# A two-layer transformer kernel: the opening of each squared-ReLU MLP by ordinary products, with moved buffers and shifted weights

## The chip, the cores and the metric

One core of a Trainium2 chip. The metric is the device time of one execution, in microseconds (us). TensorE multiplies, VectorE (DVE), ScalarE (ACT) and GpSimd (POOL) work on tiles in the on-chip memory, and DMA queues load weights. Everything is in 32-bit floats: each operand is split into a high part and a low remainder, and one product is made as three (high by high, high by low, low by high).

## What is computed

Two transformer blocks over 512 positions of 1024 features. The second, which this change touches, has two layers: an even mixer (a gated part and stick-breaking attention), then an MLP; an odd mixer (an mLSTM in chunks), then a second MLP. Cut to what matters:

```python
def _sqrelu_mlp(h, w1, w2):
    return jnp.square(jax.nn.relu(h @ w1)) @ w2

def _odd_mixer(h, w_in, conv_w, conv_b, i_b, f_b, on_g, w_out):
    p = h @ w_in
    qk = jax.nn.silu(_causal_conv(p[..., :n_qk], conv_w, conv_b))
    ...
    hc = _mlstm(q, k, v, i_pre, f_pre)
    hc = _rmsnorm(hc, on_g.reshape(C_HEADS, C_V)).astype(h.dtype)
    y = (hc * jax.nn.sigmoid(og)).reshape(bsz, seq, MIX_W)
    return y @ w_out

# each layer: x = x + mixer(rmsnorm(x, g1)); x = x + mlp(rmsnorm(x, g2))
```

w1 is 1024 x 4096 and w2 is 4096 x 1024. The norm's factor per position goes through relu and square, so it can be put on at the end.

## The kernel before

X holds the activations as eight tiles of 128 features by 512 positions, X[0] to X[7]. The program is laid out by a planner: Python writes the operations, a scheduler gives each engine its own order, and pools of tiles decide where tiles lie. A tile that takes the place of an older one waits for the older one's last reader.

A plain gemm (`gemm_t_steps`) has eight weights m of 128 outputs. `load_w` fetches each (128 x 1024), ACT makes its high part wH (L198) and DVE, or POOL where `pool_l` or `B.lean` says so, the low part wL (L200). Per weight, TensorE does 24 products of 512 columns (`mm3`, L204) into one accumulator, and the result is evacuated: for od_out, DVE adds it to X[m] (L881), for ev_out at L1264; both then take up the sum of squares `ssq` (L314).

`sq_mlp(layer)` works through four chunks c of 1024 hidden features. In a chunk there are four pairs p, each 256 hidden features by two weights, and then the gemm with w2, whose eight results are scaled and added to X (L1042, L1043). A pair is computed by a seven-product scheme: 2 x 2 blocks of weights and activations, seven products q instead of eight, each of four steps i of three products of 256 columns, 84 in all. It needs sums of weight blocks (`Pairs.weights`: tiles wH/wL, vH/vL, uH/uL with the temporary `eb`) and sums of activation blocks. Those are made once for a layer, in `Pairs.__init__`: for each i of 0 to 3 four blocks t1, t2 (X times its gain, ACT, L912), e and f (sums, DVE, L915 to L921), all split into high (ACT, L284) and low (DVE, L285): gH/gL, aH/aL, fH/fL. The results of a pair are combined on DVE, passed through relu and square on ACT (`done`), and split into the ring `hd` of eight tiles, which w2 reads.

The first pair of the first chunk, the opening, goes step by step over i, so that it can begin when i = 0 is ready. `norm` computes the norm's factor from `ssq` with one product of the row means (`pg`), behind pair 3 of chunk 0.

The pools: `hq0` and `hq1` belong to the two MLPs. `od` holds the odd mixer's tiles, among them the activations s2 and v which od_out's gemm reads, and is closed behind od_out; `hq1` is opened then and takes the same memory. `gap(pool, n)` puts a small tile into a pool, so that the tiles behind it lie 4n bytes further; `OFF = 16` moves a weight tile by 16 floats, 64 bytes.

## Time and profile before

| what | us |
|---|---|
| time, median of 3 runs | 1919.21 (1918.03 to 1919.74) |
| the profiled execution | 1916.68 |
| its span | 1914.9 |
| TensorE busy | 1855.4 (97%) |
| DVE busy | 1227.1 (64%) |
| ACT busy | 868.5 (45%) |
| POOL busy | 142.0 (7%) |

All stretches below are times from the start of the profiled execution's span. Layer 0's MLP begins where ev_out's gemm ends, near 998, layer 1's where od_out's ends, near 1555.5. A matmul's shown time is longer than the distance to the next, since matmuls are pipelined; the distance of neighbouring starts, or the chain's time over the number, is what one costs. [...]

### The profile page before, as it was taken

Reading aid. Unit: us, or ns where it says so; the run is one execution under the profiler, and the core shown is the slowest. Engines: PE = TensorE matmul, PEld = TensorE weight load, DVE = VectorE, ACT = ScalarE, POOL = GpSimd, SP = SyncE. Lnnn points to the kernel's source line nnn. Section 1 sums busy time; section 2 is a strip of 40 time slices with the busy share of each in tenths; the row PEclk is TensorE's granted clock in tenths of the full one; section 3 lists DMA queues with packets and bytes.
Section 4 is the critical chain, followed back from the end, with each engine's and each line's share of the span. In section 5 each row is a group of like instructions: output and inputs, shape, how many; then the busy total and the mean of one; then the engine's idle time right before and its main releaser. Section 6 shows DMA issues by size and latency. Waiting matters only on the chain.

```text
span 1914.9 us, 24808 instructions
## 1 busy us (share of the span) xinstructions
PE 1855.4 (97%) x9722; PEld 1533.9 (80%) x9722; DVE 1227.1 (64%) x1899; ACT 868.5 (45%) x1374; POOL 142.0 (7%) x101
## 2 busy tenths in 40 slices
PE   7999999999999999999899999999999969999999
PEld 3777788888888887776679899898777859899897
DVE  4765668664444346667878758586835577858583
ACT  2455454342323245666556344354436445445351
POOL 1000010110000002325320000001201000000000
PEclk9999999999999999999999999999999979999999
DMA  7513247522332223211122324232231213324231
GB/s 246 162 50 113 89 167 263 188 81 96 99 99 99 91 96 116 66 56 56 44 89 89 103 85 135 86 111 85 94 100 42 88 55 104 115 88 136 70 122 55
DMA packets 61652, 197.60 MB, mean 103 GB/s; under 512 B 6904, under 2 KB 8490, under 8 KB 61536
## 3 DMA queue, kind: packets, MB, share of 16 engines
q1 hardware_dynamic: 57864, 190.34, 30.5%
q10 hardware_dynamic: 3672, 5.69, 1.0%
q8 instruction: 76, 1.25, 0.3%
q14 instruction: 40, 0.33, 0.1%
HBM read 193.86 MB, written 2.15 MB: 102 GB/s over the span
## 4 chain that ended last, share of the span: by engine, by line
PE 84%; DVE 10%; ACT 4%; issue 1%; DMA 1%; SPq 0%; DVEq 0%; ACTq 0%
PE acc L204 63%; PE pm L204 15%; PE pg L204 3%; PE po L204 3%; DVE s L1395 1%; DVE sl L1315 1%; PE pm L207 1%; DVE wL L200 1%; DVE ssq L314 1%; ACT wH L198 0%; DVE aL L285 0%; DMA oh<-ada 0%; DVE vL L285 0%; DVE sq L1042 0%; ACT sz L1333 0%
## 5 line engine op out<-in xcount | busy, mean ns | idle before, releaser
L204 PE MATMUL acc<-hd,wH 128*128 128x512 f32 (+1 forms) x1552 | 474.7, 388 | 0.0
L198 ACT ACTIVATE wH<-wraw 128x1024 fp32r<-128x1024 f32 (+1 forms) x240 | 246.5, 1029 | 474.0 <-PE acc L204 399.0
L200 DVE TENSOR_TENSOR wL<-wraw,wH 128x1024 fp32r<-128x1024 f32 (+1 forms) x205 | 242.0, 1182 | 171.6 <-ACT wH L198 169.0
L204 PEld LDWEIGHTS acc<-hd,wH 128*128 128x128 f32 x1552 | 290.0, 188 | 59.6 <-issue 1.0
L204 PE MATMUL acc<-aH,wH 128*128 128x512 f32 (+1 forms) x784 | 308.5, 395 | 6.1 <-ACT aH L348 5.7
L204 PE MATMUL acc<-aL,wH 128*128 128x512 f32 (+1 forms) x784 | 303.0, 386 | 2.5 <-DVE aL L349 2.5
L204 PE MATMUL acc<-aH,wL 128*128 128x512 f32 (+1 forms) x784 | 303.0, 386 | 0.0
L204 PE MATMUL acc<-hd,wL 128*128 128x512 f32 (+1 forms) x776 | 301.1, 388 | 0.8
L204 PEld LDWEIGHTS acc<-aH,wH 128*128 128x128 f32 x784 | 148.8, 190 | 43.2 <-issue 10.3
L204 PEld LDWEIGHTS acc<-aL,wH 128*128 128x128 f32 x784 | 148.9, 190 | 32.4 <-DVE aL L349 3.4
L204 PEld LDWEIGHTS acc<-aH,wL 128*128 128x128 f32 x784 | 148.8, 190 | 30.8 <-issue 1.2
L204 PEld LDWEIGHTS acc<-hd,wL 128*128 128x128 f32 x776 | 145.7, 188 | 33.7 <-DVE wL L200 4.2
L200 POOL TENSOR_TENSOR wL<-wraw,wH 128x1024 fp32r<-128x1024 f32 x38 | 96.1, 2532 | 940.8 <-ACT wH L198 919.9
L1042 DVE TENSOR_TENSOR sq<-acc,R 128x512 f32<-128x512 f32 x63 | 43.3, 687 | 87.5 <-PE acc L204 87.3
L285 DVE TENSOR_TENSOR hd<-rl,hd 128x512 fp32r<-128x512 f32 (+1 forms) x64 | 61.1, 956 | 49.2 <-ACT hd L284 49.1
L669 DVE SCALAR_TENSOR_TENSOR X<-acc,mod,X 128x512 f32<-128x512 f32 x32 | 24.0, 751 | 83.5 <-PE acc L204 83.5
L284 ACT ACTIVATE hd<-rl 128x512 fp32r<-128x512 f32 (+1 forms) x64 | 53.8, 841 | 41.0 <-DVE rl L851 40.7
L971 ACT ACTIVATE rl<-rl 128x512 f32<-128x512 f32 x64 | 36.8, 623 | 65.5 <-DVE rl L1008 61.8
L204 PE MATMUL acc<-s,wH 128*128 128x512 f32 (+1 forms) x208 | 65.8, 375 | 0.0
L204 PE MATMUL pm<-s,s 64*128 64x384 f32 (+7 forms) x160 | 55.7, 436 | 0.0
L284 ACT ACTIVATE vH<-wraw 128x1024 fp32r<-128x1024 f32 x32 | 33.9, 1059 | 41.7 <-DVE wraw L948 32.1
L204 PE MATMUL acc<-wH,aH 128*128 128x512 f32 x120 | 50.2, 418 | 1.8 <-DVE cp L1391 1.8
(417 smaller groups left out, 3693.1 us busy)
## 6 DMA issues: line engine op xcount, KB each, us to landing
wraw<-mlp SPq DMA_DIRECT2D x128, 512.0 KB, 3.5
wraw<-w SPq DMA_DIRECT2D x64, 512.0 KB, 3.4
wraw<-ada SPq DMA_DIRECT2D x32, 512.0 KB, 4.3
wraw<-w_in SPq DMA_DIRECT2D x30, 512.0 KB, 3.9
oh<-ada SPq DMA_DIRECT2D x32, 256.0 KB, 4.7
wraw<-od_in SPq DMA_DIRECT2D x16, 512.0 KB, 3.4
wraw<-ev_in SPq DMA_DIRECT2D x12, 512.0 KB, 3.5
X<-x SPq DMA_DIRECT2D x16, 256.0 KB, 4.5
```

Source lines behind the costliest of these rows:

```text
L198: nc.scalar.activation(h[:, :n], r[:, :n], AF.Copy)
L200: (nc.gpsimd if pool_l else nc.vector).tensor_tensor(l[:, :n], r[:, :n], h[:, :n], op=OP.subtract)
L204: self.weave.placed(self.nc.tensor.matmul(out, w, x, start=start, stop=stop), out, x)
L207: self.weave.placed(self.nc.tensor.transpose(out, x, self.ident[:x.shape[0], :x.shape[0]]), out, x)
L284: nc.scalar.activation(hl[0], src, AF.Copy)
L285: nc.vector.tensor_tensor(hl[1], src, hl[0], op=OP.subtract)
L314: nc.vector.tensor_tensor(self.cur[tag], self.cur[tag], q, op=OP.add)
L669: nc.vector.scalar_tensor_tensor(X[m], acc, mod[:, 40 + m:41 + m], X[m], op0=OP.mult, op1=OP.add)
L971: nc.scalar.activation(r[:, c], r[:, c], AF.Relu, scale=sign)
L1042: nc.vector.tensor_tensor(t, acc, R2, op=OP.mult)
L1315: nc.vector.tensor_tensor(l[:, c], e[:, :w], h[:, c], op=OP.subtract)
L1395: nc.vector.scalar_tensor_tensor(y, p[:, tap:tap + NT], B.vec("convw", tap * 8 + ch), y, op0=OP.mult, op1=OP.add)
```

## The change

1. The opening becomes eight ordinary products: `Pairs.__init__` loads the two weights plainly (`u0`, moved by OFF) and only scales and splits X; `Pairs.opening` does 2 accumulators x 8 tiles x 3 products of 512 columns, with relu straight from the accumulators. `norm` comes right behind it, then `Pairs.sums` with the sums for the other pairs, which now write over t1 and t2.
2. A pool `yp` holds the ring `hd`. For layer 1 it is opened ahead of the odd mixer, and the mLSTM's temporaries `mb` and `tw` and the activations Y for od_out lie in that ring. The pool `od` is closed ahead of od_out's gemm, so that `hq1` no longer takes the memory that od_out reads.
3. w2's weight m = 7 of chunks 0 to 2 is moved by OFF (`shift`).
4. Smaller: `eb` has one buffer, the gap in `od` goes, `ev_o` sets `lean` off (the low halves of ev_out's weights behind its first group then go to DVE, not to POOL), and the operands of q = 4 to 7 are cut otherwise.

```diff
     def load_w(self, src, n=1024, pools=None, pool_h=False, pool_l=False, off=0):
...
-        h = hp.tile([P, w], F32R, name=hn, bufs=hb)
+        h = hp.tile([P, w], F32R, name=hn, bufs=hb)[:, off:]
...
-            ws = [self.load_w(srcs[i], kt * P, pool_l=i in pool_l or self.lean) for i in ms]
+            ws = [self.load_w(srcs[i], kt * P, pool_l=i in pool_l or self.lean, off=OFF if i in shift else 0) for i in ms]
...
-    sq_mlp(B, 0)
+    with ExitStack() as st:
+        sq_mlp(B, 0, st.enter_context(tc.tile_pool(name="yp0", bufs=1)))
+    st1 = ExitStack()
+    yp = st1.enter_context(tc.tile_pool(name="yp1", bufs=1))
     with ExitStack() as st:
         od = st.enter_context(tc.tile_pool(name="od", bufs=1))
...
-        Y = odd_mixer(B, od, H)
...
-        B.gemm_t([a["od_out"][m] for m in range(8)], Y, od_o, group=3)
-    sq_mlp(B, 1)
+        Y = odd_mixer(B, od, yp, H)
...
+    B.gemm_t([a["od_out"][m] for m in range(8)], Y, od_o, group=3)
+    with st1:
+        sq_mlp(B, 1, yp)
...
+        self.u0 = [B.load_w(w[b], off=OFF) for b in range(2)]
+        g = [hp.tile([P, 4, NT], F32R, name=n) for n in ("gH", "gL")]
+        self.t, self.x1, self.x2 = [], [], []
+        for i in range(4):
+            t = hp.tile([P, 1024], F32, name="rl", bufs=4)
+            for b, hl in enumerate(((g[0][:, i], g[1][:, i]), B.act_hl(2 * i))):
+                u = t[:, b * NT:b * NT + NT]
+                nc.scalar.activation(u, X[2 * i + b], AF.Copy, scale=gain(2 * i + b))
+                B.split(hl, u)
+                (self.x1, self.x2)[b].append(hl)
+            self.t.append(t)
+
+    def sums(self):
...
+            sub(t2[:, lo], t2[:, lo], t1[:, lo])
+            sub(t1[:, lo], t1[:, lo], t1[:, hi])
+            sub(t1[:, hi], t2[:, hi], t1[:, hi])
+            nc.vector.scalar_tensor_tensor(t2[:, hi], t1[:, lo], -1.0, t2[:, hi], op0=OP.mult, op1=OP.subtract)
+            sub(t2[:, lo], t1[:, hi], t2[:, lo])
             eh = B.act_hl(2 * i + 1)
-            B.split(eh, e)
+            B.split(eh, t1)
             fh = tuple(hp.tile([P, NT], F32R, name=f"f{n}{i}") for n in "HL")
...
+        B.gap(hp, 16)
...
-        eb = hp.tile([P, 1024], F32, name="eb", bufs=2)
+        eb = hp.tile([P, 1024], F32, name="eb", bufs=1)
...
+    def opening(self, w, hs):
...
+        accs = [B.acc() for _ in range(2)]
+        for i in range(4):
+            for b, x in enumerate((self.x1[i], self.x2[i])):
+                s = slice((4 * b + i) * P, (4 * b + i) * P + P)
+                for acc, (h, l) in zip(accs, self.u0):
+                    B.mm3(acc, h[:, s], l[:, s], x[0], x[1], i == b == 0, i == 3 and b == 1)
+        r = self.hp.tile([P, 1024], F32, name="rl", bufs=4)
+        for n in range(2):
+            nc.scalar.activation(r[:, n * NT:n * NT + NT], accs[n], AF.Relu)
+        self.done(r, hs, 0)
...
-            for p in range(4):
-                M.pair(w, p, hs, c == 0 and p == 0)
             if c == 0:
+                M.opening(w, hs)
                 norm()
+                M.sums()
+            for p in range(c == 0, 4):
+                M.pair(w, p, hs)
             for _ in B.gemm_t_steps([w2[c * 8 + m] for m in range(8)], hs, lambda m, acc: upd(m, acc, c == 3),
-                                    group=3, late=6, last=end if layer and c == 3 else None):
+                                    group=3, late=6, last=end if layer and c == 3 else None, shift=(7,) if c < 3 else ()):
...
     def ev_o(m, acc):
+        B.lean = False
...
-        mb = od.tile([P, NT], F32, name="mb", bufs=2)
+        mb = yp.tile([P, 1024], F32, name="hd", bufs=8)[:, :NT]
...
-            e = od.tile([P, NT], F32, name="tw", bufs=3)
+            e = yp.tile([P, 1024], F32, name="hd", bufs=8)
...
-        hl = (od.tile([P, NT], F32R, name="s2", bufs=8), od.tile([P, 576], F32R, name="v", bufs=8)[:, :NT])
+        t = yp.tile([P, 1024], F32R, name="hd", bufs=8)
+        hl = t[:, :NT], t[:, NT:]
```

In the rows below, numbers behind the names tell buffers apart; they differ between the two kernels.

TensorE where layer 0's opening begins, before: behind ev_out's last product (`acc`, aH7) come the seven-product scheme's steps for i = 0, each of 256 columns and each reading another block or sum.

```order
L204 MATMUL acc_7686<-aH7_7458,wL_7684 128x512
L204 MATMUL pm_7837<-gH_7719,wH_7818 128x256
L204 MATMUL pm_7837<-gL_7720,wH_7818 128x256
L204 MATMUL pm_7837<-gH_7719,wL_7819 128x256
L204 MATMUL pm_7838<-aH0_7733,wH_7818 128x256
L204 MATMUL pm_7838<-aL0_7734,wH_7818 128x256
```

The same place now:

```order
L204 MATMUL acc_7686<-aH7_7458,wL_7684 128x512
L204 MATMUL acc_7773<-gH_7734,wH_7724 128x512
L204 MATMUL acc_7773<-gL_7735,wH_7724 128x512
L204 MATMUL acc_7773<-gH_7734,wL_7726 128x512
L204 MATMUL acc_7774<-gH_7734,wH_7730 128x512
L204 MATMUL acc_7774<-gL_7735,wH_7730 128x512
```

The products are of 512 columns, read scaled X alone (g is X[0], X[2], ..., a0, a2, ... the others), and go on to aL6 as the last; then come norm's product and pair 1.

DVE in layer 0 now, from the end of the sums for i = 3 (L927 and L931 are the sums, L959 sums of weights, L286 the low parts). wL_7896 is the low part of pair 1's first weights, hd_7828 that of the opening's result.

```order
L931 SCALAR_TENSOR_TENSOR rl_7763<-rl_7763 128x256
L927 TENSOR_TENSOR rl_7763<-rl_7763 128x256
L286 TENSOR_TENSOR wL_7896<-wraw_7889,wH_7895 128x1024
L959 TENSOR_TENSOR wraw_7889<-wraw_7889,eb_7893 128x512
L959 TENSOR_TENSOR eb_8019<-wraw_8015,wraw_8017 128x512
L286 TENSOR_TENSOR hd_7828<-rl_7823,hd_7827 128x1024
L286 TENSOR_TENSOR aL7_7880<-rl_7763,aH7_7879 128x512
L286 TENSOR_TENSOR fL3_7884<-rl_7763,fH3_7883 128x512
```

And before, where the first weights' low part (wL_7819, the opening's own) stood in ev_out's last part, ahead of X[6]'s evacuation (X_3345):

```order
L285 TENSOR_TENSOR vL_7956<-wraw_7945,vH_7955 128x1024
L314 TENSOR_TENSOR ssq_7530<-ssq_7530,sq_7642 128x512
L285 TENSOR_TENSOR wL_7819<-wraw_7812,wH_7818 128x1024
L948 TENSOR_TENSOR wraw_7812<-wraw_7812,eb_7816 128x512
L285 TENSOR_TENSOR uL_7834<-wraw_7812,uH_7833 128x512
L1264 TENSOR_TENSOR X_3345<-X_3345,acc_7651 128x512
```

What moved: the low part that the first seven-product pair reads stands behind all sums now, 30 rows behind X[7]'s evacuation; the opening's own weights are plain ones, split ahead of that.

DVE at the end of od_out in layer 1, before (X_3345 and X_3387 are X[6] and X[7]):

```order
L881 TENSOR_TENSOR X_3345<-X_3345,acc_12578 128x512
L285 TENSOR_TENSOR wL_12877<-wraw_12870,wH_12876 128x1024
L314 TENSOR_TENSOR ssq_12457<-ssq_12457,sq_12604 128x512
L881 TENSOR_TENSOR X_3387<-X_3387,acc_12613 128x512
L135 MEMSET gap_12736 128x16
L915 TENSOR_TENSOR rl_12649<-rl_12648 128x256
L948 TENSOR_TENSOR eb_12743<-wraw_12739,wraw_12741 128x512
```

The same place now:

```order
L885 TENSOR_TENSOR X_3345<-X_3345,acc_12515 128x512
L927 TENSOR_TENSOR rl_12614<-rl_12614 128x256
L200 TENSOR_TENSOR wL_12592<-wraw_12588,wH_12590 128x1024
L931 SCALAR_TENSOR_TENSOR rl_12614<-rl_12614 128x256
L315 TENSOR_TENSOR ssq_12394<-ssq_12394,sq_12541 128x512
...
L286 TENSOR_TENSOR fL2_12731<-rl_12614,fH2_12730 128x512
L885 TENSOR_TENSOR X_3387<-X_3387,acc_12550 128x512
L286 TENSOR_TENSOR wL_12756<-wraw_12749,wH_12755 128x1024
L315 TENSOR_TENSOR ssq_12394<-ssq_12394,sq_12576 128x512
L286 TENSOR_TENSOR vL_12762<-wraw_12751,vH_12761 128x1024
L286 TENSOR_TENSOR aL6_12625<-rl_12623,aH6_12624 128x512
```

What moved: the scaled and split activations and the sums for i = 0 to 2 (up to fL2) stand ahead of X[7]'s evacuation, between od_out's; before, the first sum stood behind it.

## Rows read from the trace of the kernel before

**Rows 1.** The page: busy time, share of the span and instructions of each engine.

```profile
PE 1855.4 (97%) x9722; PEld 1533.9 (80%) x9722; DVE 1227.1 (64%) x1899; ACT 868.5 (45%) x1374; POOL 142.0 (7%) x101
```

**Rows 2.** Timeline of TensorE, layer 1: start, us, engine, line, operation, tiles.

```profile
1555.23 0.39 PE L204 MATMUL acc<-s,wL 128*128 128x512 f32 x1
...
1586.97 0.28 PE L204 MATMUL pm<-gH,wH 128*128 128x256 f32 x1
```

**Rows 3.** TensorE's waits, 1550 to 1600: us in total, times, longest.

```profile
PE pm L204 <- ACT vH L284: 14.6, 1, 14.6
PE pm L204 <- ACT gH L284: 2.4, 1, 2.4
```

**Rows 4.** Stretches: length, busy (x) of PE, PEld, DVE, ACT, POOL, granted clock, DMA share, GB/s.

```profile
955.00:998.00 43.00, 43.00 (x200) 35.20 (x197) 31.22 (x39) 18.76 (x27) 12.75 (x5) 0.96 0.26 86
998.00:1009.00 11.00, 7.29 (x35) 6.38 (x35) 10.44 (x20) 10.77 (x19) 0.00 (x0) 0.72 0.15 49
1002.90:1009.70 6.80, 6.05 (x29) 5.76 (x28) 6.80 (x15) 6.06 (x12) 0.00 (x0) 0.50 0.00 0
1015.00:1044.00 29.00, 29.00 (x256) 28.82 (x255) 27.89 (x38) 19.03 (x25) 0.00 (x0) 1.00 0.45 146
1089.00:1128.50 39.50, 39.50 (x337) 39.50 (x336) 30.15 (x39) 21.99 (x29) 0.00 (x0) 1.00 0.34 107
1520.00:1555.50 35.50, 35.50 (x158) 29.16 (x156) 16.63 (x20) 11.27 (x14) 0.00 (x0) 1.00 0.24 74
1555.50:1579.70 24.20, 5.47 (x22) 4.60 (x22) 23.87 (x46) 17.00 (x30) 0.00 (x0) 0.58 0.11 33
1559.20:1579.70 20.50, 4.89 (x20) 4.30 (x21) 20.43 (x39) 13.51 (x24) 0.00 (x0) 0.50 0.13 39
```

**Rows 5.** Timeline of TensorE, layer 0: the opening's first products, and pair 2's first.

```profile
997.82 0.28 PE L204 MATMUL pm<-gH,wH 128*128 128x256 f32 x1
...
998.05 0.28 PE L204 MATMUL pm<-gH,wL 128*128 128x256 f32 x1
...
1025.10 0.28 PE L204 MATMUL pm<-gH,wH 128*128 128x256 f32 x1
```

**Rows 6.** The chain: start, us, engine, tile, line, number; pairs, norm, gemm.

```profile
1025.27 5.44 PE pm L204 x48
...
1044.31 0.86 PE pg L204 x2
...
1089.14 5.66 PE pm L204 x48
...
1539.98 15.65 PE acc L204 x69
```

**Rows 7.** DVE's timeline and the chain at the end of od_out.

```profile
1555.65 0.69 DVE L881 TENSOR_TENSOR X<-X,acc 128x512 f32<-128x512 f32 x1 [2.75 <-PE acc L204]
1555.71 0.73 ACT rl L912
```

**Rows 8.** Timeline of DVE, layer 0: neighbours of 1024, 512 and 256 columns.

```profile
1002.17 1.22 DVE L285 TENSOR_TENSOR wL<-wraw,wH 128x1024 fp32r<-128x1024 f32 x1
1003.31 0.68 DVE L285 TENSOR_TENSOR aL<-rl,aH 128x512 fp32r<-128x512 f32 x1
1003.91 0.42 DVE L285 TENSOR_TENSOR gL<-rl,gH 128x256 fp32r<-128x256 f32 x1
1004.24 0.42 DVE L915 TENSOR_TENSOR rl<-rl 128x256 f32<-128x256 f32 x1
```

**Rows 9.** A wait of TensorE and its stretch, and another stretch at half clock.

```profile
1393.45 0.50 PE L204 MATMUL acc<-wH,aH 128*128 128x512 f32 x1 [1.79 <-DVE cp L1391]
1391.00:1398.00 7.00, 5.21 (x23) 3.98 (x23) 6.41 (x9) 2.29 (x3) 0.00 (x0) 1.00 0.40 121
405.50:408.90 3.40, 3.40 (x18) 3.40 (x18) 3.05 (x9) 2.56 (x7) 0.00 (x0) 0.51 0.31 119
```

**Rows 10.** TensorE's waits in the mLSTM, 1434 to 1476.

```profile
PE po L207 <- ACT num L1472: 1.3, 3, 0.6
```

More of the change, by code (lines that the diff above doesn't have):

```diff
@@ L221, in gemm_n, with gemm_t_steps @@
             pass
-    def gemm_t_steps(self, srcs, xs, evac, group=1, kt=KT, pool_l=(), ks=None, halves=False, last=None, late=None):
+    def gemm_t_steps(self, srcs, xs, evac, group=1, kt=KT, pool_l=(), ks=None, halves=False, last=None, late=None, shift=()):
         m = 0
@@ L902, in __init__ @@
+    def sums(self):
+        B, hp, nc = self.B, self.hp, self.B.nc
         lo, hi = HALVES
         self.x = []
[L904 to L907 removed]
+        cut = lambda hl, c: tuple(t[:, c] for t in hl)
         for i in range(4):
[L909 to L921 removed]
@@ L924, in __init__ @@
             fh = tuple(hp.tile([P, NT], F32R, name=f"f{n}{i}") for n in "HL")
[L925 to L928 removed]
+            B.split(fh, t2)
+            self.x.append({1: cut(self.x1[i], lo), 2: cut(self.x2[i], lo), 3: cut(self.x2[i], hi),
+                           5: cut(eh, lo), 7: cut(eh, hi), 4: cut(fh, lo), 6: cut(fh, hi)})
@@ L977, in done, with pair @@
             hs[2 * p + n] = h[:, c], l[:, c]
-    def pair(self, w, p, hs, opening=False):
+    def opening(self, w, hs):
+        B, nc = self.B, self.B.nc
+        accs = [B.acc() for _ in range(2)]
[8 more added lines that the diff above has]
+        self.done(r, hs, 0)
+    def pair(self, w, p, hs):
         B, nc = self.B, self.B.nc
@@ L984, in pair @@
         u = self.weights(w, p)
[L985 to L988 removed]
+        x, y, z, v = B.pm2(), B.pm2(), (B.pg, B.pout)[p % 2](), B.acc()
+        ps = {1: x[:, lo], 7: x[:, hi], 2: y[:, lo], 6: y[:, hi], 5: z[:, lo], 3: v[:, lo], 4: v[:, hi]}
+        for q in (1, 2, 6, 7, 5, 3, 4):
             for i in range(4):
[L990 to L998 removed]
+                self.mm(ps[q], u, q, i)
         r = self.hp.tile([P, 1024], F32, name="rl", bufs=4)
@@ L1002, in pair, with sq_mlp @@
         twice = lambda t: t[:, None, :].to_broadcast([P, 2, half])
-        def add(out, x, q, q2=None):
-            if q2 is None:
-                nc.vector.tensor_tensor(out, x, ps[q], op=OP.add)
-            elif q in pairs:
-                nc.vector.tensor_tensor(out, x, pairs[q], op=OP.add)
-            else:
-                for n, k in enumerate((q, q2)):
-                    nc.vector.tensor_tensor(out[:, n * half:n * half + half], x[:, n * half:n * half + half], ps[k], op=OP.add)
-        nc.scalar.activation(at(3), ps[1], AF.Copy)
-        if opening:
-            add(at(0), at(3), 2)
-            add(at(1), at(3), 6)
-        else:
-            nc.vector.tensor_tensor(two(at(0, 2)), twice(at(3)), two(y), op=OP.add)
-        add(at(2), at(1), 7)
-        out = bass.AP(tensor=r.tensor, offset=r.offset + half, ap=[r.ap[0], [2 * half, 2], [1, half]])
-        nc.vector.tensor_tensor(out, two(at(1, 2)), twice(ps[5]), op=OP.add)
-        add(at(1, 2), at(1, 2), 3, 4)
+        add = lambda out, a, b: nc.vector.tensor_tensor(out, a, b, op=OP.add)
+        nc.scalar.activation(at(3), ps[1], AF.Copy)
+        add(two(at(0, 2)), twice(at(3)), two(y))
+        add(at(2), at(1), ps[7])
+        out = bass.AP(tensor=r.tensor, offset=r.offset + half, ap=[r.ap[0], [2 * half, 2], [1, half]])
+        add(out, two(at(1, 2)), twice(ps[5]))
+        add(at(1, 2), at(1, 2), v)
+        for n, sign in enumerate((1.0, -1.0)):
+            c = slice(n * NT, n * NT + NT)
+            nc.scalar.activation(r[:, c], r[:, c], AF.Relu, scale=sign)
         self.done(r, hs, p)
-def sq_mlp(B, layer):
+def sq_mlp(B, layer, yp):
     nc, tc, a, X = B.nc, B.tc, B.a, B.X
```

67 lines of the change are left out of this document (15 added, 52 removed).

## The prediction

> **What bounds the kernel now.** I read the page's busy times first, then the chain that ended last, then TensorE's waits by stretch, then tables of stretches, and single rows last. TensorE is busy for 97% of the span [rows 1], and the chain runs through it nearly everywhere. So two things can shorten the run: time in which TensorE stands idle or at the lower clock, and the time that its products take one behind another. DVE and ACT matter only where they are late for it.
>
> The two MLP openings are places where they are late. In layer 1 the last product of od_out starts at 1555.23 [rows 2], and from 1555.5 TensorE is idle for 24.20 - 5.47 = 18.7 us [rows 4], of which 2.4 and 14.6 us are two single waits [rows 3]. [...] In layer 0 TensorE is idle for 11.00 - 7.29 = 3.7 us from 998, and the clock is 0.50 for 6.8 us [rows 4], and from the opening's first product at 997.82 to pair 2's at 1025.10 [rows 5] go 27.3 us for two pairs.
>
> The third place is the pace. 48 products of 256 columns take 5.44 us in chunk 0 and 5.66 us in chunk 1 [rows 6], at a granted clock of 1.00 in both [rows 4]: 113.3 against 117.9 ns a product, 9.52 against 9.90 us a pair of 84. All of chunks 1 to 3 of both layers show the second pace (24 pairs; [rows 4] has one such chunk, 337 products in 39.5 us), all of chunk 0 behind the clock's return the first. A gemm's products of 512 columns take 15.65/69 = 226.8 ns [rows 6], exactly twice 113.4.
>
> **Layer 1, the waits.** The sums and all that comes behind them start when od_out has ended: ACT's first `rl` at 1555.71 [rows 7], DVE's sums after it, though X[0] had been final since od_out's first weights. What held them is the place of their tiles, which lie where od_out's activations lay. The change takes those out of the way, and the order shows the consequence: the copies, splits and sums for i = 0 to 2 now stand between od_out's evacuations, on ACT and on DVE. There is room: DVE is busy 16.6 of the 35.5 us before od_out's end [rows 4]. From neighbouring starts, a DVE operation of 256, 512 and 1024 columns takes 0.33, 0.60 and 1.14 us [rows 8]. Between two evacuations od_out's products take 24 x 0.2268 = 5.44 us, and the new rows there come to between 5.1 and 5.8 us; od_out's accumulators are several, so I count no stall. From the last evacuation, 1555.7, DVE needs 0.6 + 1.14 + 0.6 + 1.14 + 0.6 = 4.1 us up to the last split that the opening reads (aL6), so 1560 to 1560.5. The opening needs it as the last of its eight operands, at 1555.45 + 42 x 0.2268 = 1565: 4.5 us to spare. Pair 1's sums end near 1567 and are first read near 1570.
>
> So the opening runs from 1555.45 for 48 x 0.2268 = 10.9 us. That is 1.4 us more than a pair of 84 at the good pace, the price of doing without the seven-product form. norm's one product takes half of 0.86 us for two of the kind [rows 6], 0.43 us; it stood behind pair 3 and now stands here. Pair 1 starts at 1566.8 instead of 1586.97, and 0.43 us is not paid later: **20.6 us less**. The lower-clock stretch goes with the idle time that stood before it.
>
> **Layer 0.** Here the tiles were never in the way, and the work itself is late: DVE is busy 27.9 of 29.0 us behind the opening [rows 4]. The opening needs none of the sums, so its waits go: 48 products from 997.82 to 1008.7, norm to 1009.1. But the low half of pair 1's first weights (wL_7896) stands behind all sums of i = 0 to 3 in DVE's new order, and these behind X[7]'s evacuation, which can start near 998.15 (ev_out's last product starts 0.23 us before the opening's first; layer 1's evacuation came 0.42 us behind the start of its last [rows 2, 7]). Twenty operations of 256 columns, ten of 512 and that split of 1024 follow from there: 998.15 + 6.7 + 6.0 + 1.14 = 1012.0. TensorE waits for it at pair 1's third product, from 1009.4: **2.6 us, a wait in place of the removed ones**. Pair 1 ends at 1012.0 + 82 x 0.1134 = 1021.3; before, the same point was 1025.10 [rows 5]. That gives 3.8 + 0.4 = 4.2 us, unless the clock drops again. A wait of 1.79 us elsewhere left the clock at 1.00, and the wait of 2.4 us in layer 1 stood before a drop [rows 3, 4, 9]; 2.6 is nearer to the second. A stretch at 0.50 was 3.4 us in the shortest case and 6.8 us in another [rows 4, 9], and costs half of it: 1.7 to 3.4 us. I take 2.5, so **1.7 us less**, with 0.8 to 4.2 as ends.
>
> ev_o now turns `lean` off, so that ev_out's later weight splits move from POOL, where five took 12.75 us, to DVE at 1.14 us each. DVE is busy 31.2 of the 43 us before 998 [rows 4]; five splits take 5.7 of the 11.8 that are free, and I count no wait of TensorE for them.
>
> **The mLSTM stage.** Its temporaries `mb` and `tw` move into the ring of eight hd tiles, one ring where there were two of two and three: more room, with other neighbours. TensorE's only wait there sums to 1.3 us [rows 10]. I take 0.5 us less; ends are 1.3 less and 1.0 more.
>
> **The shifted weights.** In the program's layout the weights of a pair begin 64 bytes past a multiple of 128 and the activations at a multiple; all other products have both at a multiple. The change gives w2's last weight of chunks 0 to 2, and the two of the opening, the pairs' place. The trace has no 512-column product laid out so, and the price must be bounded. What it does have: pairs that follow directly on unshifted products at 1.00 have 117.9 ns, all chunks 1 to 3 and the first three products of layer 0's opening, 0.23 us from the first to the third [rows 5]; pairs that follow on a stretch at 0.50 have 113.3. The layout is the same in both, so the pace is something that is entered and then kept, and the boundary decides. If entering from shifted products at 1.00 gives the good pace, 24 pairs gain 0.38 us each: **9.1 us less**. If not, 0, and pairs 1 to 3 of layer 1 lose the good pace which the lower clock gave them: 1.1 us more. For the eight shifted stretches themselves, 6 x 5.44 + 2 x 10.9 = 54 us, I bound the change at the ratio of the paces, 4%, 2.2 us either way, and take 0. I take the gain: the good pace also outlasts brief waits, and what precedes it is then never unshifted work at 1.00.
>
> [...]
>
> The rest is nothing: `eb` with one buffer instead of two makes its next writer wait for readers that stand ahead of it on its own engine and on ACT, and the simpler evacuation issues the same operations for the pairs that already had it. Cover: DVE is busy 30 of 39.5 us in a chunk's pairs [rows 4], and the good pace leaves 38.1.
>
> **The sum.** The profiled run is 1916.7 (span 1914.9, 1.8 around it); the median of the runs is 1919.2, 2.5 above. 1916.7 - 20.6 - 1.7 - 0.5 - 9.1 = 1884.8, and with 2.5 the forecast is **1887**.
>
> **The rivals.**
> 1. The shift has no effect: every pair behind an opening and behind w2 runs at 117.9 ns. 1916.7 - 20.6 - 1.7 - 0.5 + 1.1 + 2.5 = **1897.5**. For it: no row shows a shifted product of 512 columns change anything. Against: the good pace exists in the same layout.
> 2. Layer 0's wait comes out otherwise, with the shift working: without a lower-clock stretch 4.2 instead of 1.7, **1885**; with 6.8 us of it and a wait that is some 2 us longer, **1890**.
> 3. Slower: DVE's sums hold up od_out. DVE runs in order, and an evacuation that stands behind sums holds its accumulator. If the new rows between evacuations came to more than 5.44 us by enough to use up the free accumulators, od_out's eight weights would be stretched, and all of the 18.7 us could come back inside od_out, with the lower clock, the ordinary products' 1.4 us in each layer, and rival 1's 1.1 us: 1919.2 + 2.8 + 1.1 = **1923**, if layer 0 gives nothing either. It decides from about 8 us of DVE work between evacuations; the rows give 5.1 to 5.8. The same price holds if the hq1 tiles still waited for od_out, which the order speaks against.
>
> **How the numbers follow.** The forecast with its layer-0 variants (rival 2) has 0.60: 0.45 and 0.15. Rival 1 has 0.31, rival 3 has 0.03, and 0.06 is for something in between, part of layer 1's wait left (1900 to 1912). The range reaches over rivals 1 and 2 with the bounds of the shifted stretches and of mLSTM: from 1883 (no lower-clock stretch, 1.3 in mLSTM, some of the 2.2) to 1900 (rival 1 with 2.2 more). About 0.2% (3.8 us) is what a measurement can tell from no change; faster by more 0.96, within 0.01, slower 0.03.
>
> **What would show it.** In the profile after: no TensorE wait above 1 us behind od_out, and pair 1 of layer 1 some 11.3 us behind its last product; in layer 0 one wait of 2 to 3 us for DVE's wL at pair 1, with or without a clock of 0.50 behind it; 48 products of 256 columns in 5.44 us in chunks 1 to 3 for the forecast, in 5.66 for rival 1. The prediction is wrong if TensorE waits inside od_out, or if pairs in chunks 1 to 3 take some third time.

## The result and the profile after

The changed kernel takes **1897.24 us** (median of four runs, 1894.02 to 1898.91) against 1918.62 before (1917.37 to 1919.74): ratio 0.9887, 95% interval 0.987 to 0.9904. It is faster by 21.4 us. The forecast was 1887, its first rival 1897.5, the range 1883 to 1900: right in direction and inside the range, 10 us off in the number. The profiled execution of the changed kernel took 1898.35 and that of the kernel before 1916.68, so the traces stand 18.3 us apart, 3 us less than the medians. All stage times below are of one profiled execution of each kernel.

Where the difference lies, in us from the start of the span, by the first product of each stage on TensorE (before, layer 1 is counted from 1555.5, where od_out's products end, since its opening begins with a wait):

| stage | before | after | difference |
|---|---|---|---|
| up to layer 0's opening | 997.8 | 997.1 | -0.7 |
| layer 0: opening, norm, pairs of chunk 0 | 46.8 | 44.8 | -2.0 |
| layer 0: the rest of the MLP, up to w2 of chunk 3 | 251.0 | 251.1 | +0.1 |
| w2 of chunk 3, odd mixer, od_out | 259.9 | 263.8 | +3.9 |
| layer 1: opening, norm, pairs of chunk 0 | 60.5 | 40.6 | -19.9 |
| the rest, up to the last product | 295.1 | 295.2 | +0.1 |

The 0.7 us of the first line lie ahead of ev_out, in parts that the change does not touch; ev_out itself takes 38.9 us in both, so that its weight splits on DVE cost TensorE nothing.

First the page of the changed kernel, for [rows 1]:

```profile
PE 1855.5 (98%) x9650; PEld 1530.9 (81%) x9650; DVE 1217.3 (64%) x1887; ACT 865.4 (46%) x1368; POOL 129.8 (7%) x96
```

and TensorE's waits from 990 to 1600 (engine, tile, line, what it waited for; us in total, times, longest), for [rows 3, 10]:

```profile
PE acc L204 <- DVE cp L1396: 3.1, 1, 3.1
PE pm L204 <- DVE wL L286: 2.3, 1, 2.3
PE po L207 <- ACT num L1476: 0.9, 2, 0.5
```

TensorE is busy as long as before; what went is idle time. The 14.6 and 2.4 us of layer 1 are gone, and the list is now headed by two waits for DVE: one in the odd mixer for `cp`, 3.1 us where before it was 1.8 [rows 9], and the one forecast in layer 0, for `wL`.

The stretches of the changed kernel (length; busy time of PE, PEld, DVE, ACT, POOL; granted clock as a share; DMA share, GB/s), for [rows 4]. In the traces, products of 256 columns start 213 ns apart at 0.50 (before: 15 of them in 3.20 us from 1006.12) and 113 to 118 ns apart at 1.00:

```profile
1012.30:1015.80 3.50, 3.50 (x19) 3.50 (x18) 3.47 (x6) 3.50 (x6) 0.00 (x0) 0.51 0.00 0
1086.10:1125.60 39.50, 39.50 (x337) 39.50 (x336) 31.37 (x41) 21.63 (x28) 0.00 (x0) 1.00 0.36 119
1391.20:1398.10 6.90, 5.94 (x14) 4.68 (x15) 5.70 (x8) 3.54 (x6) 0.98 (x2) 0.51 0.25 77
1520.00:1556.80 36.80, 36.80 (x164) 30.47 (x163) 30.26 (x51) 24.35 (x36) 0.00 (x0) 1.00 0.31 101
1556.80:1568.00 11.20, 11.20 (x49) 9.02 (x48) 11.20 (x20) 5.65 (x9) 0.00 (x0) 1.00 0.31 94
```

The fourth line is od_out: DVE is busy 30.3 of 36.8 us there, where it was 16.6 of 35.5, and TensorE all the time. The sums have moved under it and held nothing up. The fifth is layer 1's opening, without a gap and at a granted clock of 1.00. Two short stretches at 0.51 remain, each behind one of the two waits. And the second line has 337 products in 39.5 us, exactly as before: **the pace of the pairs in chunks 1 to 3 did not change**.

The chain of the changed kernel shows the pace at the start of chunk 1 of layer 0, and of layer 1 in chunk 0 (start, us, engine, tile, line, number), for [rows 6]:

```profile
1086.20 5.66 PE pm L204 x48
...
1569.03 5.47 PE pm L204 x48
...
1578.58 5.44 PE pm L204 x48
```

So 5.66 us for 48 in chunk 1, right behind w2's shifted weight, but 5.44 in chunk 0 of layer 1, where no stretch at the lower clock lies ahead any more. Neither my forecast nor my first rival has both.

### The profile page after: what moved, and what is told of

Read it like the earlier page. It is cut to its first block, busy times and chain, and to the rows that moved or that the text cites. A ratio compares the mean times of both kernels' runs of the same rounds, so it can differ in the third digit from the quotient of the medians.

```text
span 1896.4 us, 24622 instructions
## 1 busy us (share of the span) xinstructions
PE 1855.5 (98%) x9650; PEld 1530.9 (81%) x9650; DVE 1217.3 (64%) x1887; ACT 865.4 (46%) x1368; POOL 129.8 (7%) x96
## 4 chain that ended last, share of the span: by engine, by line
PE 85%; DVE 9%; ACT 3%; issue 1%; DMA 1%; SPq 0%; DVEq 0%; ACTq 0%
PE acc L204 65%; PE pm L204 14%; PE po L204 3%; PE pg L204 3%; DVE s L1400 1%; DVE wL L200 1%; DVE sl L1320 1%; PE pm L207 1%; DMA oh<-ada 1%; ACT wH L198 0%; DVE ssq L315 0%; DVE sq L1044 0%; ACT sz L1338 0%; ACT se L1316 0%; DVE rl L927 0%
## 5 line engine op out<-in xcount | busy, mean ns | idle before, releaser
L204 PE MATMUL acc<-hd,wH 128*128 128x512 f32 (+1 forms) x1680 | 513.9, 388 | 0.0
L204 PEld LDWEIGHTS acc<-hd,wH 128*128 128x128 f32 x1680 | 313.9, 188 | 64.1
L200 DVE TENSOR_TENSOR wL<-wraw,wH 128x1024 fp32r<-128x1024 f32 (+1 forms) x214 | 252.2, 1183 | 156.7 <-ACT wH L198 150.1
L204 PE MATMUL acc<-hd,wL 128*128 128x512 f32 (+1 forms) x840 | 326.3, 388 | 0.8
L204 PE MATMUL acc<-aH,wH 128*128 128x512 f32 (+1 forms) x800 | 315.1, 395 | 6.2 <-ACT aH L349 5.8
L204 PE MATMUL acc<-aL,wH 128*128 128x512 f32 (+1 forms) x800 | 309.2, 387 | 2.5 <-DVE aL L350 2.5
L204 PE MATMUL acc<-aH,wL 128*128 128x512 f32 (+1 forms) x800 | 309.1, 386 | 0.0
L204 PEld LDWEIGHTS acc<-hd,wL 128*128 128x128 f32 x840 | 157.8, 188 | 36.5 <-DVE wL L200 4.2
L200 POOL TENSOR_TENSOR wL<-wraw,wH 128x1024 fp32r<-128x1024 f32 x33 | 83.3, 2527 | 603.5 <-ACT wH L198 582.5
L286 DVE TENSOR_TENSOR hd<-rl,hd 128x512 fp32r<-128x512 f32 (+1 forms) x64 | 61.2, 958 | 56.7 <-ACT hd L285 56.7
L285 ACT ACTIVATE wH<-wraw 128x1024 fp32r<-128x1024 f32 x30 | 31.7, 1061 | 41.3 <-issue 19.5
```

The source lines that it names most:

```text
L200: (nc.gpsimd if pool_l else nc.vector).tensor_tensor(l[:, :n], r[:, :n], h[:, :n], op=OP.subtract)
L204: self.weave.placed(self.nc.tensor.matmul(out, w, x, start=start, stop=stop), out, x)
L285: nc.scalar.activation(hl[0], src, AF.Copy)
L286: nc.vector.tensor_tensor(hl[1], src, hl[0], op=OP.subtract)
```

## Experiments

The stages are read as in the table: a "chunk" is four pairs, and the w2 stage ahead of it contains whatever stands between. In the changed kernel a w2 stage of chunks 0 to 2 takes 44.11 and a chunk 39.57 us, 83.68 together.

### What brings the good pace

My theory after the result: the shift of w2 does nothing, and what differs in layer 1's chunk 0 is norm's product, which stands between the opening and pair 1. It is the only one there that works in full 32-bit floats (two entries of the trace for one product, 0.86 us in the chain at 1568.17), while all others run on the split parts.

**e5_norm_late**, norm back behind pair 3:

```diff
                 M.opening(w, hs)
-                norm()
                 M.sums()
...
                 M.pair(w, p, hs)
+            if c == 0:
+                norm()
```

> The changed kernel with norm's product behind pair 3 again, so that pair 1 follows directly on the shifted opening. Theory B: pairs 1 to 3 of layer 1 go from 5.44 to 5.66 us for 48 (layer 0's keep 5.44, since there TensorE waits and the clock drops ahead of them). Rival D (the shifted opening brings the good pace): layer 1's stay at 5.44.

The chain of this kernel, layer 1, pairs 1 and 2:

```profile
1568.29 5.65 PE pm L204 x48
...
1578.18 5.65 PE pm L204 x48
```

The pace is gone, in pairs that follow directly on 48 shifted products at a granted clock of 1.00. In layer 0 of the same kernel, where a wait and a stretch at 0.50 lie ahead, the pairs have 113 ns without norm's product. **e4_open_plain** is the counterpart, with the opening's weights unshifted:

```diff
-        self.u0 = [B.load_w(w[b], off=OFF) for b in range(2)]
+        self.u0 = [B.load_w(w[b]) for b in range(2)]
```

> The changed kernel with the opening's two weights unshifted. Theory B (norm's product behind the opening breaks the run): pairs 1 to 3 of layer 1 stay at 5.44 us for 48. Rival D (48 shifted products of the opening bring the good pace, 24 of w2's last weight are too few): they go to 5.66, 1.1 us more in that stage.

```profile
1567.56 5.46 PE pm L204 x48
...
1577.10 5.44 PE pm L204 x48
```

The pace stays. Rival D falls: in layer 1 what stands ahead was not shifted here and the pace came (5.44 us), and without norm's product it did not (5.65 in e5). The opening itself takes 10.88 us here and 11.20 in the changed kernel: a shifted product of 512 columns costs 233 instead of 227 ns.

**e1_no_shift**, w2's last weight unshifted:

```diff
-                                    group=3, late=6, last=end if layer and c == 3 else None, shift=(7,) if c < 3 else ()):
+                                    group=3, late=6, last=end if layer and c == 3 else None):
```

> The changed kernel with w2's last weight of chunks 0 to 2 back at its unshifted place; all else as changed. Theory A (the shift of w2 does nothing for the pairs that follow and costs a little in w2): pairs of chunks 1 to 3 stay at 5.66 us for 48 products, and the six w2 stages go from 44.11 back to 43.95 us, so about 1 us less than the changed kernel. Rival (the shift gives something that the stage table hides): 1 to 9 us more.

Pairs 39.57 us a chunk, as with the shift; w2 stages 43.95, as before the change. By the stages the shift costs 0.16 us in each of six, 1 us in all. The whole time, 1898.98 (1897.37 to 1899.99; ratio 0.9896, 0.9881 to 0.9911), cannot show so little: runs of one kernel lie up to 5 us apart.

**e2_break**, a product like norm's ahead of each chunk:

```diff
+            if c:
+                B.mm(B.pout(), B.colD.to_broadcast([P, P]), R2)
             for p in range(c == 0, 4):
                 M.pair(w, p, hs)
```

> The changed kernel with one more product ahead of the pairs of chunks 1 to 3, of norm's kind (512 columns, full 32-bit, result not used). Theory B (the good pace is entered when the run of products is broken by one of another kind): pairs of chunks 1 to 3 go from 5.66 to 5.44 us for 48, 1.5 us a chunk, and the product costs 0.85, so 6 x 0.65 = 4 us less. Theory C (only a stretch at a granted clock of 0.50, or the opening itself, brings the good pace): the pace stays, and the time is 6 x 0.85 = 5 us more.

Timeline of TensorE at the start of chunk 1, layer 0:

```profile
1089.29 0.39 PE L204 MATMUL acc<-hd,wL 128*128 128x512 f32 x1
1089.52 1.02 PE L204 MATMUL po<-R,colD 128*128 128x512 f32 x2
1089.97 0.68 PE L204 MATMUL pm<-gH,wH 128*128 128x256 f32 x1
1090.49 0.28 PE L204 MATMUL pm<-gL,wH 128*128 128x256 f32 x1
```

and the stretch behind it:

```profile
1090.50:1128.20 37.70, 37.70 (x335) 37.70 (x334) 29.69 (x39) 20.70 (x28) 0.00 (x0) 1.00 0.37 116
```

335 products in 37.7 us, 112.5 ns by the count at the window's edges, 113.4 from start to start: the good pace in all six chunks. The price is to be read in the starts: 0.45 us for the product and 0.52 instead of 0.12 for the first product behind it. A chunk with its w2 stage takes 38.51 + 44.56 = 83.07, 0.61 less than in the changed kernel, and 1894.14 us in all (1891.23 to 1896.52; 0.9866, 0.985 to 0.9883). Behind w2, theory B holds in these six chunks, and theory C falls.

**e3_break64_plain** tried it cheaper, 64 columns instead of 512, with no shift anywhere (the edits of e1 and e4, and `R2[:, :64]`):

> The changed kernel with neither w2's weight nor the opening's weights shifted, and a breaking product of 64 columns instead of 512 ahead of the pairs of chunks 1 to 3 (result not used). Theory B, by the runs before (the shift costs 0.16 us in each of six w2 stages and 0.32 in each opening; a broken run gives pairs at 5.44 us for 48): a w2 stage and the four pairs behind it take 43.95 + 38.1 + about 0.25 for the short product, 82.3 against 83.68 in the changed kernel, so 6 x 1.4 + 0.6 = 9 us less than the changed kernel. If the break's length or the shift matters after all (rival), the pairs stay at 39.57 and the gain is 1.6 less the products.

A miss. A chunk takes 39.66 us:

```profile
1087.10:1126.40 39.30, 39.30 (x336) 39.30 (x335) 31.08 (x41) 21.28 (x28) 0.00 (x0) 1.00 0.35 118
```

The good pace did not come (1897.2 us, 1895.21 to 1898.86). So the break must have a size, or the shift matters after all. **e10_break_kinds** put a different break ahead of each of the six chunks, without any shift:

```diff
+            if c:
+                d = B.pout()
+                n, k = {(0, 1): (128, 1), (0, 2): (256, 1), (0, 3): (384, 1), (1, 1): (0, 1), (1, 2): (64, 8), (1, 3): (128, 4)}[layer, c]
+                for j in range(k):
+                    if n:
+                        B.mm(d[:, j * n:j * n + n], B.colD.to_broadcast([P, P]), R2[:, j * n:j * n + n])
+                    else:
+                        B.mm(d, M.x1[0][0][:, :P], M.x1[0][0])
```

> The changed kernel without any shift, with six different breaks ahead of the pairs of chunks 1 to 3 (results not used): layer 0 one full 32-bit product of 128, 256, 384 columns; layer 1 one of the same kind as all others, 512 columns; eight full 32-bit products of 64; four of 128. A 512-column one brought 5.44 us for 48 products, a 64-column one left 5.66. If the length of the break decides, the pace turns to 5.44 somewhere between 128 and 384, and the eight and the four, each as long as one of 512, bring it too. If it is the kind (a change of kind with a wide product), only the wide ones do, and the eight of 64 do not. A product of the same kind should leave 5.66 in either case; if it brings 5.44, any odd product between would do.

Stretches of the six chunks, in the order of the program:

```profile
1088.00:1126.40 38.40, 38.40 (x328) 38.40 (x328) 30.81 (x41) 21.05 (x28) 0.00 (x0) 1.00 0.36 119
1172.00:1209.40 37.40, 37.40 (x332) 37.40 (x331) 29.90 (x39) 20.84 (x28) 0.00 (x0) 1.00 0.36 122
1254.60:1292.10 37.50, 37.50 (x333) 37.50 (x332) 29.80 (x39) 20.73 (x28) 0.00 (x0) 1.00 0.38 119
1641.30:1680.00 38.70, 38.70 (x331) 38.70 (x330) 31.07 (x41) 21.13 (x28) 0.00 (x0) 1.00 0.37 121
1726.60:1764.20 37.60, 37.60 (x334) 37.60 (x334) 28.74 (x38) 20.50 (x27) 0.00 (x0) 1.00 0.33 111
1809.50:1847.10 37.60, 37.60 (x334) 37.60 (x333) 29.65 (x39) 20.56 (x28) 0.00 (x0) 1.00 0.36 116
```

Length over number: 117 ns for one product of 128 columns, 113 for 256 and 384, 117 for a 512-column product of the same kind as all others, 113 for eight of 64 and for four of 128. Between w2 and the pairs the turn thus went with the length of the break in full 32-bit products, not with the width of one: one of 128 was too short, 256 was enough, and four of 128 did it too. A 512-column product of the common kind did nothing. No change of the clock came with it: all six chunks are at 1.00. Each of these six kinds stands in one chunk of one execution; more rests on 64 columns (all six chunks of e3 stay), on 512 (all six of e2 turn) and on 256 (all twelve of e11 and e12, below, turn).

The break is not a law, though, and other traces show that. In e9, described below, layer 1's pair 0 runs at 118 ns, norm's product of 512 full 32-bit columns stands behind it, and pair 1 goes on at 118 (chain: the product, then 48 of pair 1):

```profile
1575.21 1.05 PE pg L204 x2
1576.26 5.65 PE pm L204 x48
```

There the break stands behind 256-column products that already had the worse pace; everywhere else that pairs follow one, it stands behind 512-column ones. Nor did a wait with a stretch at 0.50 behind it always end at one pace. Twelve MLP openings of these runs have such a stretch: eight came out of it at 113 ns (both of before, layer 0 of the changed kernel and of e1 to e5), four at 118 (layer 1 of e8 and of e9, layer 0 of e10 and of e12). In e8 the pairs even had 113 ns behind norm's product until the wait, and 118 from there on. In e12, pair 2 of layer 0:

```profile
1024.31 5.65 PE pm L204 x48
```

And in e6 pair 1 of layer 0 comes out of its wait, at a clock of 1.00, at 118 ns; behind one product that takes 147 ns, with no wait shown, it goes on at 113. So only a halt of some 30 ns stood ahead of the turn there, where 128 full 32-bit columns brought none in e10. What sets the pace is open: the runs show where a break turned it, not why.

### Which part of the change took layer 1's wait

**e8_pools_back**: the pools of layer 1 as before, the opening ordinary (the ring opened behind od_out, `mb`, `tw` and Y in `od`, `od` closed behind od_out's gemm). The main part of the edit:

```diff
-    B.gemm_t([a["od_out"][m] for m in range(8)], Y, od_o, group=3)
-    with st1:
-        sq_mlp(B, 1, yp)
+        B.gemm_t([a["od_out"][m] for m in range(8)], Y, od_o, group=3)
+    with ExitStack() as st1:
+        sq_mlp(B, 1, st1.enter_context(tc.tile_pool(name="yp1", bufs=1)))
...
```

> The changed kernel with part 2 undone for layer 1: the hd ring opened behind od_out, mb, tw and Y in od again, od closed behind od_out's gemm; the opening stays ordinary. If the pools alone put the work between od_out's evacuations, ACT's and DVE's first work starts behind od_out again; the ordinary opening hides part of it, and pair 1 waits for DVE, whose rows up to fL3 then sum to about 24 us behind 1557: pair 1 ends some 10 us later than in the changed kernel, 8 to 13 with the lower clock, so the pools are worth about half of layer 1's gain and the opening the other half. Rival (the opening alone is what hides it): less than 3 us later.

**e9_seven_l1** is the other half: pools as changed, layer 1's opening by the seven-product form.

```diff
-            if c == 0:
+            if c == 0 and layer == 0:
...
-            for p in range(c == 0, 4):
+            if c == 0 and layer:
+                M.sums()
+            for p in range(c == 0 and layer == 0, 4):
                 M.pair(w, p, hs)
+                if c == 0 and layer and p == 0:
+                    norm()
```

> The changed kernel with layer 1's opening made by the seven-product form again (sums ahead of it, norm behind pair 0), pools as changed. With the pools alone the sums for i = 0 to 2 lie under od_out, and DVE's rows behind X[7]'s evacuation sum to some 8 us up to fL3, which pair 0 needs near 4 us behind its start: TensorE waits about 4 us, perhaps with the clock at 0.50 behind it (1.7 to 3.4 more), and saves 1.4 to 1.7 of columns; layer 1's opening and chunk 0 take 40.65 + 2 to 6 us. Rival (DVE holds back od_out's evacuations, since the opening's weights now need sums as well): od_out's stage itself is longer.

TensorE's waits from 1545 to 1610, the two largest of e8 and then the two largest of e9:

```profile
PE pm L204 <- DVE vL L286: 5.6, 1, 5.6
PE acc L204 <- ACT gH L285: 2.6, 1, 2.6
```

```profile
PE pm L204 <- ACT fH L285: 4.0, 1, 4.0
PE pm L204 <- ACT aH L285: 0.8, 1, 0.8
```

and the stage of opening, norm and chunk 0 in e8 (from the opening's first product, behind the wait of 2.6 us), in e9 and in the changed kernel:

```profile
1553.70:1607.40 53.70, 47.72 (x303) 43.80 (x303) 47.60 (x76) 35.72 (x53) 0.00 (x0) 0.88 0.29 89
```

```profile
1556.30:1605.80 49.50, 44.08 (x340) 42.58 (x339) 42.58 (x59) 27.70 (x38) 0.00 (x0) 0.93 0.34 107
```

```profile
1556.80:1597.40 40.60, 40.60 (x303) 37.93 (x302) 35.37 (x49) 25.74 (x36) 0.00 (x0) 1.00 0.36 117
```

To set e8 beside the 60.5 us of before, its first wait has to be counted in, as it is there: from the end of od_out's products, 1550.9, it is 56.5 us. So 60.5 us before, 56.5 with the opening alone, 49.5 with the pools alone, 40.6 with both. In e8 the first wait is ACT's `gH` again: the tiles still wait for od_out. In e9 the work lies under od_out, but DVE and ACT are not through when pair 0 wants the f sums. The two parts are worth 4.0 and 11.0 us alone and 19.9 together. In both, the waits that are left still come with a lower clock (means of 0.88 and 0.93 in the stretches above), which with both parts is gone. Each of the two kernels ran once, in 1908.32 and 1906.53 us.

Both expectations were too low. In e8 pair 1 ends 15 us later than in the changed kernel, counted from od_out's end, where I had expected 8 to 13: with the opening in place, the pools are worth 15.9 of the 19.9 us, and not half. e9's 8.9 us above the changed kernel are more than the 2 to 6 that I had expected: beside the 4.0 us there are 0.8, 0.3 and 0.3, the stretch at 0.50 was 6.8 us long, and pairs 1 to 3 stayed at 118 ns, another 1.1 us.

### The wait in the odd mixer

**e6_tw_three**: the mLSTM's `tw` in three tiles of the ring, taken once:

```diff
+    EB = [yp.tile([P, 1024], F32, name="hd", bufs=8) for _ in range(3)]
     for h in range(4):
...
-            e = yp.tile([P, 1024], F32, name="hd", bufs=8)
+            e = EB[(4 * h + i) % 3]
```

> The changed kernel with the mLSTM's tw limited to three tiles, taken once from the hd ring and used in turn, so that its exponentials can't run ahead. Theory E (with eight tiles four of tw's operations move into the gate and convolution work on DVE and hold up an evacuation there): TensorE's wait near 1389 goes from 3.1 back to about 1.8 us, no stretch at 0.50 behind it, 1.3 to 4.7 us less than the changed kernel. Rival (the order ahead of the wait is set by something else in the change): the wait stays at 3.1.

DVE's timeline ahead of the wait in the changed kernel, three operations of `tw` (here in tiles named hd, L1450) among the convolution's (L1400), ahead of the evacuation `cp` that TensorE waits for:

```profile
1388.72 0.47 DVE L1450 TENSOR_SCALAR hd<-hd,gcol 128x512 f32<-128x512 f32 x1
1389.11 0.74 DVE L1400 SCALAR_TENSOR_TENSOR s<-cp,vecs,s 128x512 f32<-128x512 f32 x1
1389.78 0.41 DVE L1450 TENSOR_SCALAR hd<-hd,gcol 128x384 f32<-128x384 f32 x1
1390.11 0.94 DVE L1400 SCALAR_TENSOR_TENSOR s<-cp,vecs,s 128x512 f32<-128x512 f32 x1
1390.97 0.54 DVE L1450 TENSOR_SCALAR hd<-hd,gcol 128x256 f32<-128x256 f32 x1
1391.43 0.68 DVE L1396 TENSOR_TENSOR cp<-acc,R 128x512 f32<-128x512 f32 x1
```

In the kernel before, nothing of `tw` stands there; the convolution's three operations (L1395) follow one another, and then comes `cp`:

```profile
1390.47 2.32 DVE L1395 SCALAR_TENSOR_TENSOR s<-cp,vecs,s 128x512 f32<-128x512 f32 x3
1392.71 0.68 DVE L1391 TENSOR_TENSOR cp<-acc,R 128x512 f32<-128x512 f32 x1
```

In e6 the same wait, and a stretch behind it:

```profile
PE acc L204 <- DVE cp L1396: 2.0, 1, 2.0
1391.20:1394.50 3.30, 3.30 (x9) 2.60 (x8) 2.97 (x5) 1.12 (x2) 0.00 (x0) 0.50 0.20 34
```

With `mb` and `tw` back in their own two rings (e8) it is 1.8, and no stretch at 0.50 follows. So it is the greater number of free tiles that let `tw` run ahead on DVE; e6 takes back 1.1 of the 1.3 us. The rest of the expectation failed: 3.4 us at 0.50 still follow the shorter wait. The whole time, 1896.65 (1894.99 to 1897.96; 0.9893, 0.9876 to 0.9909), does not stand out from the changed kernel (ratio 0.9887): the wait is 1.1 us shorter, but the waits for `num` rose from 0.9 to 2.2 us.

### Layer 0's wait

**e7_w1_first**: pair 1's weights ahead of the sums, the opening's result behind them (the heart of the edit).

```diff
...
                 norm()
+                u1 = M.weights(w, 1) if layer == 0 else None
                 M.sums()
+                M.done(r0, hs, 0)
...
```

> The changed kernel with pair 1's weights of layer 0 split ahead of the sums, and the opening's result split behind them. If only the place of wL in DVE's order makes the wait of 2.3 us, it goes, and the stretch at 0.50 with it: 4 us less. If DVE's whole work up to the last sum sets the end (its rows sum to 998.2 + 16.2 = 1014.4 for fL3, needed near 1012.6), the wait moves to pair 1's products with f and is about 1.8 us: some 0.5 less, and 1.7 more less if the clock then stays at 1.00.

The wait for wL went; TensorE stops for 0.6 and 0.3 us at the f sums instead, with no lower clock: chunk 0 of layer 0 takes 31.6 us behind norm where the changed kernel has 33.2. But the total is 1898.22 (1896.04 to 1899.32), and the stretches of chunk 1, layer 0 and layer 1, say why:

```profile
1084.90:1125.00 40.10, 40.10 (x337) 40.09 (x336) 31.44 (x41) 21.89 (x28) 0.00 (x0) 1.00 0.37 118
1641.60:1681.10 39.50, 39.50 (x335) 39.41 (x334) 31.62 (x41) 21.75 (x29) 0.00 (x0) 1.00 0.37 120
```

My edit had put layer 0's weight tiles ahead of the 64-byte gap, so that vH, vL, uH and uL of layer 0 lay at a multiple of 128 bytes. Chunks 1 to 3 of layer 0 then take 40.11 us instead of 39.57, 119.4 ns a product; layer 1, whose layout was untouched, keeps its pace. The 119.4 is a mean of a pair's 84 products: with 118 ns for the 24 with wH and wL, which still lie 64 bytes further, it leaves 120 for the 60 with the tiles that moved, an estimate. An accident, but it shows what the place of the weights was worth here, 0.54 us a chunk.

### The sum of it

**e12_break256** is the changed kernel with the break of 256 columns and, by the edits of e1 and e4, no shift; **e11_all** has beside that e6's and e7's edits, with the gap laid ahead of the weights.

```diff
+            if c:
+                B.mm(B.pout()[:, :256], B.colD.to_broadcast([P, P]), R2[:, :256])
             for p in range(c == 0, 4):
```

> The changed kernel with only the breaking product of 256 columns and no shift: 6 x 1.16 + 0.6 = 7.6 us less than the changed kernel, near 1889; the layer-0 wait and the one near 1389 stay as in the changed kernel.

> All that the runs pointed to, on the changed kernel: no shift of w2 or of the opening; a breaking product of 256 columns ahead of the pairs of chunks 1 to 3 (result not used); tw in three tiles; in layer 0 pair 1's weights split ahead of the sums, with the 64-byte gap laid ahead of them so that they keep the pairs' place. A chunk's pairs and w2 take 38.28 + 44.23 against 83.68: 6 x 1.16 = 7 us less; the openings 0.6 less; the wait near 1389 1.1 less; layer 0's wait 2.3 down to about 1.3 and no stretch at 0.50 behind it, 1 to 2.7 less. Together 10 to 11 us less than the changed kernel, near 1886. Rival: what is gained in the pairs comes back as DVE's waits, since pairs at the good pace leave it 38.3 us a chunk: then the pairs show waits and less than 5 us are gained.

e12: **1890.68 us** (1889.48 to 1892.12; ratio 0.9853, 0.984 to 0.9867). e11: **1886.27** (1884.64 to 1888.42; 0.9829, 0.9816 to 0.9843), 11 us below the changed kernel and 32 below before. A stretch of chunk 1 in e11, and its waits in layer 0 and the odd mixer:

```profile
1087.70:1125.80 38.10, 38.10 (x338) 38.07 (x337) 30.49 (x41) 21.22 (x28) 0.00 (x0) 1.00 0.35 122
```

```profile
PE acc L204 <- DVE cp L1406: 2.0, 1, 2.0
PE pm L204 <- DVE fL L286: 1.1, 2, 0.6
```

38.28 + 44.2 us for a chunk and its w2 stage, and in chunks 1 to 3 no wait of the pairs for DVE; the total is the one expected. e12's lies 1.7 us above its own, and in its profiled execution the 118 ns in layer 0 cost some 1 us.

## Why the prediction was right, and where it was wrong

**Layer 1, the waits** (20.6 us less): right, 19.9. No wait was left behind od_out, and e8 and e9 show both halves of the mechanism. Pair 1 starts 11.66 us behind the opening's first product instead of 11.3. The terms mis-sized are the opening, 11.20 for 10.9, because a shifted 512-column product was slower (233 ns against 227 in e4), and norm, whose product also delays the next by 0.4 us. Its 0.43 us came out right (0.45) by luck: the x2 of [rows 6] that the prediction halved is one product in two entries, whose shown times overlap.

**Layer 0** (1.7 less): right, 2.0. The wait came where it was put, at pair 1's third product for wL, 2.29 us against 2.6, and was followed by 3.4 us at the lower clock, which cost 1.7 where 2.5 had been taken; the opening and norm took back the rest. The length of that stretch is luck: in e6, e8 and e9, whose layer 0 is built the same, the same wait left the clock at 1.00. Nor does the length of a wait decide, by which the prediction chose: in e6 one of 2.0 us stands before a stretch at 0.50, and one of 2.3 us does not. No run undid layer 0's opening alone.

**The mLSTM stage** (0.5 less, ends 1.3 less and 1.0 more): wrong, 3.9 more in the profiled run. I had looked for the price of the moved tiles in the mLSTM, where TensorE's wait indeed fell from 1.3 to 0.9, with two new ones of 0.3 and 0.2. I had not asked what else DVE does when `tw` finds free tiles earlier. The step that failed is "more room, with other neighbours": with more room in the ring, `tw` started sooner on DVE, on which TensorE waits. That is 1.3 us of waiting (3.1 against 1.8; 2.0 with three tiles in e6), and behind it 6.8 us at the lower clock, of which half is lost; in e12, which has the wait without that stretch, the stage loses about 1 us (260.8, against 259.9), which is within the ends given.

**The shifted weights** (9.1 less): wrong. The step that failed is the choice between two readings of the same rows. Pairs behind a stretch at 0.50 had the good pace, pairs behind unshifted products at 1.00 had not; I concluded that the layout of the products ahead decides. By e1 the shift of w2 does nothing for the pairs, and by e4 and e5 what gave layer 1 its pace is norm's product. In e2 and e10 to e12 a break of 256 full 32-bit columns or more behind w2 turned the pace from 117.8 to 113.4 ns, where 64 in e3 and 128 in e10 did not, but e9 has a break of 512 that did not, and what sets the pace stays open. The rows of before could not decide it: layer 1's norm stood behind its chunk 0 and ahead of w2, where no pair could show it. That the pace is "entered and then kept" was right within a run of products; that it "outlasts brief waits" holds in layer 0 of before, where it is 113 ns ahead of and behind halts of up to 0.16 us near 1013.7 and 1018.2, but e8 lost it in its wait of 5.6 us. The bound of 4% on a shifted 512-column product was right too, but not the value of 0 within it: 2.9% more in the opening, 1.6 us in all, with w2's six.

In the traces the sum is off by 13.5 us, of which 9.1 are the shift and 4.4 the odd mixer; the other errors cancel. The median is off by only 10 because the 2.5 us by which the median of before lay above its profiled execution were added, while the changed kernel's median lies 1.1 below its own. That is luck too.

The first rival's 1897.5 lies beside the median by errors that cancel: it has layer 1's pairs lose the good pace (1.1 us more), which norm's new place prevents, it has nothing for the shift's 1.6 us, and it has the odd mixer 0.5 less, where it is some 1 to 4 more.

## What to carry to other kernels

In these kernels the pairs' products of 256 columns had 117.8 ns behind w2, and 113.4 behind a break of 256 or more full 32-bit columns (e2, e11, e12). Where a trace shows two paces for one shape at one granted clock, look for what last stood between, try a product of another kind there, and read the pace in every stretch behind it, since a break did not always turn it here (e9). Before a wait is put down to an operation's cost, ask which tiles it waits for: taking the tiles out of the way and taking the sums out of the opening were worth 11.0 and 4.0 us alone and 19.9 together. And a temporary in a bigger ring ran ahead on DVE here, and TensorE's wait for what stood behind it went from 1.8 to 3.1 us: look at what stands behind such a temporary on its engine.
